# Seven block products instead of eight in the value projections of a two-layer trunk

## The chip, the cores and the metric

The kernel runs on one core of one Trainium2 chip. Its time is the device time of one execution in microseconds (us), and smaller is better. TensorE (PE) multiplies matrices, VectorE (DVE) and ScalarE (ACT) work elementwise, GpSimd (POOL) and SyncE (SP) mostly issue DMAs. Each engine runs its own instructions in the order in which the compiler wrote them down, and waits on semaphores for the others.

## The reference, cut to what matters

The model has two layers. Each adds a token mixer, a cross-attention on a memory and a squared-ReLU MLP to `x` (256 tokens, 2048 features). The part that changes is the attention:

```
h, mem_n = rms_norm(x, g_xattn[i]), rms_norm(mem, g_mem[i])        # 256 x 2048 each
q = (h @ w_q).reshape(.., 4 heads, 512)
k, v = split(mem_n @ w_kv, 2)                                      # v: 256 x 2048 = mem_n @ w_v
p = softmax(q k^T * 512**-0.5)                                     # per head, 256 x 256
x = x + (p v) @ w_o
```

The MLP is `x + square(relu(h @ w_up)) @ w_down`, with 8192 hidden features. All is float32.

## The kernel before, in words

**Number format.** Every float32 weight and activation is split in two parts of TensorE's faster float32 form: `split` lets ACT cast the high part (line 101, tile `whi` for weights) and DVE subtract it from the source (line 102, `wlo`). A product of two such numbers is three matmuls: high by high, high by low, low by high.

**Weights.** They stream from memory in chunks of 128 x 1024 floats (512 KB), loaded by SP into `wraw` (4 buffers, `wload`, line 118) and split by `wtile` into `whi` and `wlo` (3 buffers each). A chunk holds two k tiles of 128 by 512 output features (`KB = 2`), or, for the projections with transposed output (`gemm_feat`, used for q, k and the MLP's first matrix), four k tiles by 256 features (`FK = 4`).

**Plain product.** `gemm_tok` computes 256 tokens by 512 features: 8 chunks, 12 matmuls of 512 columns for each (2 k tiles, 2 token tiles, 3 parts). The value projection is four calls of it, one for each head; after each, the result is scaled by the memory's norm and split into `vh` and `vl` (lines 536 and 537) and weighted by the softmax of its head (24 matmuls of 256 columns, line 547), which gives `oT`.

**Seven-product form.** `gemm_seven` computes 256 tokens by two blocks of 512 features at once. For the first two chunks of each block (a 2 by 2 by 2 block product: two token tiles, two chunks, two feature blocks) it uses the scheme with seven block products instead of eight, each of 6 matmuls. It needs sums of the activation blocks (`token_sums`, lines 645 to 648, then a split) and of the weight blocks: DVE subtractions of two 128 x 1024 tiles (lines 718, 724, 729, 734), each split again. Products are numbered 1 to 7. The other six chunks of each block are plain (`direct`, 12 matmuls each). The code writes the products down as 5, 1, 2, a direct, 6, a direct, 7, a direct, 4, a direct, 3, then directs; `keep` (line 710) copies intermediate results out of PSUM, and `gather` adds results to `x`. Raw weights of the four special chunks are loaded into `ws`; the tile `run` holds the running difference of products 5, 6 and 4, while `ws` keeps the sources. The form is used for `w_o` in both attentions (two calls each) and for `w_down` in layer 1's MLP (seven calls).

**Order of the work.** The order on each engine is set at compile time by a scheduler that lets the work written down first go first, unless its inputs are not ready in its own model of time. `at(n, fn)` writes `fn` down n steps (`tick`, one for each weight chunk of a plain product) later. `mem_prep` prepares the transposed, scaled memory (`memT`) in four pieces as side work under the q projection of head 0; the k projection that follows reads its k tiles from 0 to 15.

Of the kernel before, what the change touches and what calls it, by code (L numbers as in the profile page):

```python
# [35 lines left out]
MAGIC = 12582912.0  # L36


class Trunk:
# [114 lines left out]
    def gemm_feat(self, act, w, n, dst):  # L154
# [4 lines left out]
        for kc in range(KT // FK):  # L159
            hi, lo = self.wtile(w, n, kc)  # L160
            for kk in range(FK):
                kt = kc * FK + kk
                st, en = kt == 0, kt == KT - 1
# [109 lines left out]
    def mem_prep(self, pool, layer):  # L273
# [192 lines left out]
    def attention(self, x, layer, cur, nxt):  # L466
# [3 lines left out]
        with tc.tile_pool(name="at", bufs=2, reuse_waits="tile") as ap:  # L470
# [5 lines left out]
            def proj(act, w, n, nm):  # L476
                h = ap.tile([P, 4, S], F32R, name=nm + "h")
                l = ap.tile([P, 4, S], F32R, name=nm + "l")
                for i in range(2):
                    z = ap.tile([P, 2, S], F32, name="z")  # L480
                    self.gemm_feat(act, w, 2 * n + i, z)
# [37 lines left out]
            for hd in range(HEADS):  # L519
                q = proj(hT, wq, hd, "q")  # L520
                self.flush()
                k = proj(memT, wk, hd, "k")
# [7 lines left out]
            for hd in range(HEADS):  # L530
                acc = self.gemm_tok(memT, wv, hd)
                vh = ap.tile([P, 2, HD], F32R, name="vh")
                vl = ap.tile([P, 2, HD], F32R, name="vl")
                for t in range(2):
                    r = self.rstd_mem[:, t:t + 1]
                    nc.scalar.activation(out=vh[:, t, :], in_=acc[:, t, :], func=AF.Copy, scale=r)
                    nc.vector.scalar_tensor_tensor(out=vl[:, t, :], in0=acc[:, t, :], scalar=r,
                                                   in1=vh[:, t, :].bitcast(F32), op0=ALU.mult, op1=ALU.subtract)
# [15 lines left out]
                if hd == 0:  # L554
                    for fp in range(2):
                        o = ap.tile([P, 2, S], F32, name="o", tag="e")
                        nc.scalar.copy(out=o, in_=ops[fp])
                        ops[fp] = o
                    sums = self.token_sums(ap.tile([P, KB * NB], F32, name="s", tag="qh"),
                                           lambda: ap.tile([P, 4, 2, P], F32R, name="sums", tag="kh"), *ops)  # L560

            nxt.start()
            count = iter(range(100))
            ws = lambda: ap.tile([P, KB * NB], F32, name="ws", tag=("ql", "qh")[next(count) % 2])
            run = lambda: ap.tile([P, KB * NB], F32, name="run", tag="kl")
            pair = {}

            def kept(i):
                if i in (1, 2):
                    return ap.tile([P, NB], F32, name="kept", tag="z")  # L570
                if i == 0:
                    pair[0] = ap.tile([P, 2, NB], F32, name="kept2", tag="kl")
                return pair[0][:, i // 3, :]
# [5 lines left out]
            for j in range(0, NCH, 2):  # L579
                self.gemm_seven((ws, run, kept), lambda kt, t: [f[:, kt, t * P:(t + 1) * P] for f in oT[:2]],  # L580
                                sums, wo, j, 0, gather)
# [4 lines left out]
    def mlp(self, x, layer, cur, nxt):  # L586
# [3 lines left out]
        with tc.tile_pool(name="ml", bufs=4, reuse_waits="tile") as mp:  # L590
            r2 = mp.tile([P, 32 if layer else 56], F32, name="r2", bufs=1)[:, 0:2]
            ws = lambda: mp.tile([P, KB * NB], F32, name="ws", bufs=4)
            sm = lambda: mp.tile([P, 4, 2, P], F32R, name="sums", bufs=2)
            run = lambda: mp.tile([P, KB * NB], F32, name="run", bufs=1)
            kept = lambda i: mp.tile([P, NB], F32, name="kept", bufs=4)
            for b in range(DFF // D):
                hid = []
                for n in range(NCH):
# [3 lines left out]
                    for i in range(2):  # L602
                        r = mp.tile([P, 2, S], F32, name="r", bufs=2)
# [5 lines left out]
                    if nxt.closing and n == 0:  # L609
                        sums = self.token_sums(ws(), sm, *rs)  # L610
# [11 lines left out]
                for n in range(NCH):  # L622
                    end = b == DFF // D - 1
                    if nxt.closing and not (end and n >= NCH - 2):
                        if n % 2 == 0:
                            self.gemm_seven((ws, run, kept), lambda kt, t: [f[:, kt % 4, t * P:(t + 1) * P]
                                                                            for f in hid[kt // 4]],
                                            sums, wd, n, b * KT, gather)
# [24 lines left out]
    def gemm_seven(self, tiles, token, sums, w, n0, k0, gather):  # L653
# [6 lines left out]
        kc0 = k0 // KB  # L660
        ws, run, kept = tiles
        raw, half = {}, lambda t: t.rearrange("p (k c) -> p k c", k=KB)

        def fetch(i, j):
            t = ws()
            self.fed = nc.sync.dma_start(out=half(t), in_=w[n0 + j, kc0 + i]).ins
            raw[i, j] = t
# [7 lines left out]
        begun = set()  # L675

        def into(key, kts, left, hi, lo, end=False):
            out = banks[key]
            for kk in kts:
                ah, al = left(kk)  # L680
                mm = lambda s, m, e: nc.tensor.matmul(out, s, m, start=key not in begun, stop=e, skip_group_check=True)  # L681
                mm(ah, hi[:, kk, :], False)
                begun.add(key)
                mm(ah, lo[:, kk, :], False)
                mm(al, hi[:, kk, :], True)

        def block(key, t, i, src, end=False):
            into(key, range(KB), lambda kk: token(KB * i + kk, t), *parts(src), end)

        def summed(key, k, src, end=False):  # L690
            into(key, range(KB), lambda kk: [f[:, k, kk, :] for f in sums], *parts(src), end)

        todo = {j: list(range(2, KT // KB)) for j in range(2)}

        def direct(j, first):
# [3 lines left out]
            for t in (first, 1 - first):  # L699
                into((t, j), range(KB), lambda kk: token(KB * kc + kk, t), hi, lo)  # L700
                yield
            self.tick()

        def whole(*a):
            for _ in direct(*a):
                pass
# [5 lines left out]

        acc = [self.psA.tile([P, 2, NB], F32, name="acc") for _ in range(2)]
        banks = {(1, 0): acc[0][:, 0], (0, 1): acc[0][:, 1], (0, 0): acc[1][:, 0], (1, 1): acc[1][:, 1]}
        for i, j in ((0, 0), (0, 1), (1, 0), (1, 1)):
            fetch(i, j)
        run = run()
        v.tensor_tensor(out=run, in0=raw[0, 1], in1=raw[0, 0], op=ALU.subtract)
        summed((0, 1), 0, run, True)
        block((1, 0), 0, 0, raw[0, 0], True)  # L720
        m5, m1 = keep((0, 1), 0), keep((1, 0), 1)
        block((0, 0), 0, 1, raw[1, 0])
        whole(1, 1)
        v.tensor_tensor(out=run, in0=raw[1, 1], in1=run, op=ALU.subtract)
        summed((1, 0), 1, run, True)
        gather(0, n0, m1)
        u2 = keep((1, 0), 2)
        whole(1, 1)
        v.tensor_tensor(out=raw[0, 1], in0=raw[1, 1], in1=raw[0, 1], op=ALU.subtract)
        summed((1, 0), 2, raw[0, 1], True)  # L730
        gather(0, n0 + 1, u2)
        u3 = keep((1, 0), 3)
        whole(0, 0)
# [667 lines left out]
```

## Time and profile before

| | |
|---|---|
| time, median of 3 runs | 2835.14 us (2832.22 to 2835.55) |
| profiled execution, its own time | 2834.88 us |
| its span, first to last instruction | 2832.0 us |
| TensorE busy | 2798.7 us (99%) |
| VectorE busy | 1958.4 us (69%) |
| ScalarE busy | 1393.7 us (49%) |
| mean granted TensorE clock | 0.998 of 2.4 GHz |

Matmuls are pipelined and their ends are modelled: a matmul's "busy" or mean time is not the time by which the next one is held up. What counts is the distance from one start to the next. In the chain of waits a line "20.20 PE acc L149 x89" is 89 matmuls that started one after the other within 20.20 us.

### The profile page before, as it was taken

Reading aid. Unit: us, or ns where it says so; the run is one execution under the profiler, and the core shown is the slowest. Engines: PE = TensorE matmul, PEld = TensorE weight load, DVE = VectorE, ACT = ScalarE, POOL = GpSimd, SP = SyncE. Lnnn points to the kernel's source line nnn. Section 1 sums busy time; section 2 is a strip of 40 time slices with the busy share of each in tenths; the row PEclk is TensorE's granted clock in tenths of the full one; section 3 lists DMA queues with packets and bytes.
Section 4 is the critical chain, followed back from the end, with each engine's and each line's share of the span. In section 5 each row is a group of like instructions: output and inputs, shape, how many; then the busy total and the mean of one; then the engine's idle time right before and its main releaser. Section 6 shows DMA issues by size and latency. Waiting matters only on the chain.

```text
span 2832.0 us, 39687 instructions
## 1 busy us (share of the span) xinstructions
PE 2798.7 (99%) x15172; PEld 2346.5 (83%) x15172; DVE 1958.4 (69%) x2707; ACT 1393.7 (49%) x1801; POOL 200.3 (7%) x374
## 2 busy tenths in 40 slices
PE   9999999999999999999999999999999999999998
PEld 7888888888888888888777788888888888888886
DVE  6855655578878788787567666556676767667665
ACT  5545544454544444444455445444454545445453
POOL 0100000001022222222011000000000000000000
PEclk9999999999999999999999999999999999999999
DMA  8766665657677777777879766566556576575755
GB/s 287 238 199 204 193 180 186 180 156 237 195 220 215 224 223 220 217 223 211 236 249 286 217 213 200 175 187 192 171 179 217 163 223 186 170 217 163 221 160 155
DMA packets 180847, 579.55 MB, mean 205 GB/s; under 512 B 37440, under 2 KB 39664, under 8 KB 179888
## 3 DMA queue, kind: packets, MB, share of 16 engines
q1 hardware_dynamic: 142304, 513.34, 59.0%
q0 software_dynamic: 38208, 63.62, 8.3%
q8 instruction: 118, 1.93, 0.3%
q14 instruction: 73, 0.60, 0.1%
q10 hardware_dynamic: 144, 0.07, 0.0%
HBM read 553.88 MB, written 22.94 MB: 204 GB/s over the span
## 4 chain that ended last, share of the span: by engine, by line
PE 88%; DVE 4%; DMA 4%; issue 2%; ACT 1%; POOL 0%; DVEq 0%; POOLq 0%; SPq 0%; ACTq 0%
PE acc L166 23%; PE acc L149 21%; PE acc L681 14%; PE acc L168 12%; PE acc L766 4%; PE acc L765 4%; PE acc L764 4%; DVE wlo L102 2%; DMA Kd<-kd 1%; PE ps L547 1%; PE ps L490 1%; DMA wraw<-in_f_w_down 1%; PE ps L149 1%; ACT whi L101 1%; PE ps L217 1%
## 5 line engine op out<-in xcount | busy, mean ns | idle before, releaser
L102 DVE TENSOR_TENSOR wlo<-wraw,whi 128x1024 fp32r<-128x1024 f32 x908 | 1108.5, 1222 | 660.8 <-ACT whi L101 656.8
L101 ACT CAST whi<-wraw 128x1024 fp32r<-128x1024 f32 x908 | 955.0, 1052 | 1128.6 <-PE acc L166 360.3
L166 PE MATMUL acc<-act,whi 128*128 128x512 f32 x3072 | 1082.9, 396 | 0.9 <-ACT whi L101 0.8
L168 PE MATMUL acc<-act,wlo 128*128 128x256 f32 x3072 | 865.0, 282 | 1.7 <-DVE wlo L102 1.5
L166 PEld LDWEIGHTS acc<-act,whi 128*128 128x128 f32 x3072 | 576.0, 188 | 133.9 <-ACT whi L101 1.7
L149 PE MATMUL acc<-whi,act 128*128 128x512 f32 x1984 | 623.5, 393 | 8.6 <-ACT whi L101 6.9
L168 PEld LDWEIGHTS acc<-act,wlo 128*128 128x128 f32 x3072 | 580.4, 189 | 7.0 <-DVE wlo L102 3.4
L149 PEld LDWEIGHTS acc<-whi,act 128*128 128x128 f32 x1984 | 373.0, 189 | 86.6 <-ACT whi L101 6.9
L149 PE MATMUL acc<-wlo,act 128*128 128x512 f32 x992 | 387.7, 391 | 2.0 <-DVE wlo L102 2.0
L149 PEld LDWEIGHTS acc<-wlo,act 128*128 128x128 f32 x992 | 187.0, 189 | 40.5 <-DVE wlo L102 2.9
L765 PE MATMUL acc<-wlo,hh 128*128 128x512 f32 x544 | 215.1, 395 | 0.2 <-DVE wlo L102 0.2
L764 PE MATMUL acc<-whi,hh 128*128 128x512 f32 x544 | 214.5, 394 | 0.0
L766 PE MATMUL acc<-whi,hl 128*128 128x512 f32 x544 | 214.4, 394 | 0.0
L681 PE MATMUL acc<-wlo,hh 128*128 128x512 f32 x378 | 147.6, 390 | 1.7 <-DVE wlo L102 1.6
L681 PE MATMUL acc<-whi,hh 128*128 128x512 f32 x378 | 147.6, 390 | 0.5
L681 PE MATMUL acc<-whi,hl 128*128 128x512 f32 x378 | 147.2, 389 | 0.0
L681 PE MATMUL acc<-whi,act 128*128 128x512 f32 x432 | 135.8, 389 | 0.0
L765 PEld LDWEIGHTS acc<-wlo,hh 128*128 128x128 f32 x544 | 102.2, 188 | 24.4 <-DVE wlo L102 1.5
L766 PEld LDWEIGHTS acc<-whi,hl 128*128 128x128 f32 x544 | 102.2, 188 | 22.8 <-issue 1.6
L764 PEld LDWEIGHTS acc<-whi,hh 128*128 128x128 f32 x544 | 102.2, 188 | 22.2 <-issue 0.4
L681 PEld LDWEIGHTS acc<-whi,act 128*128 128x128 f32 x432 | 80.8, 188 | 16.7 <-ACT kept L710 0.2
L681 PEld LDWEIGHTS acc<-wlo,hh 128*128 128x128 f32 x378 | 71.0, 188 | 17.9 <-DVE wlo L102 3.1
(320 smaller groups left out, 2562.5 us busy)
## 6 DMA issues: line engine op xcount, KB each, us to landing
wraw<-in_f_w_up SPq DMA_DIRECT2D x256, 512.0 KB, 4.2
wraw<-in_f_w_down SPq DMA_DIRECT2D x228, 512.0 KB, 4.3
wraw<-in_a_w_in SPq DMA_DIRECT2D x64, 512.0 KB, 4.5
wraw<-in_x_w_q SPq DMA_DIRECT2D x64, 512.0 KB, 3.7
wraw<-in_x_w_k SPq DMA_DIRECT2D x64, 512.0 KB, 3.7
wraw<-in_x_w_v SPq DMA_DIRECT2D x64, 512.0 KB, 3.7
wraw<-in_b_w_out SPq DMA_DIRECT2D x64, 512.0 KB, 4.4
wraw<-in_x_w_o SPq DMA_DIRECT2D x48, 512.0 KB, 3.9
```

What stands on the lines that cost most here:

```text
L101: self.nc.scalar.copy(out=hi, in_=src)
L102: self.nc.vector.tensor_tensor(out=lo, in0=src, in1=hi.bitcast(F32), op=ALU.subtract)
L149: nc.tensor.matmul(out[t], pairs[m][0][:, kt, sl], pairs[m][1][:, kk, :], start=st and m == 0, stop=en and m == 2)
L166: nc.tensor.matmul(acc[:, f, :], hi[:, kk, sl], both[:, kt].rearrange("p a s -> p (a s)"), start=st, stop=False, skip_group_check=True)
L168: nc.tensor.matmul(acc[:, f, 0:S], lo[:, kk, sl], ah[:, kt, :], start=False, stop=en, skip_group_check=True)
L217: nc.tensor.transpose(pt[:, kk, t * P:(t + 1) * P], src[:, t, c:c + P], self.ident)
L490: mm = lambda s, m, b, e: nc.tensor.matmul(sc[:, t, :], s, m, start=b, stop=e, skip_group_check=True)
L547: mm = lambda s, mv, b, e: nc.tensor.matmul(op[:, k, :], s, mv, start=b, stop=e, skip_group_check=True)
L681: mm = lambda s, m, e: nc.tensor.matmul(out, s, m, start=key not in begun, stop=e, skip_group_check=True)
L764: nc.tensor.matmul(acc[:, t, :], ah[:, kt % 4, sl], hi[:, kk, :], start=st, stop=False)
L765: nc.tensor.matmul(acc[:, t, :], ah[:, kt % 4, sl], lo[:, kk, :], start=False, stop=False)
L766: nc.tensor.matmul(acc[:, t, :], al[:, kt % 4, sl], hi[:, kk, :], start=False, stop=en)
```

## The change

The value projections of both attentions use the seven-product form too, two heads per call, with the activation sums of the memory (`mem_sums`). `gemm_seven` is replaced by `gemm_pair`, which takes the order of the products as a list and an optional function `end` for the finished blocks. What differs:

- Product 1 comes before product 5; the directs come in another order at the end of the list.
- The tile `run` is gone: each weight difference is written over a raw chunk, 5, 6 and 4 over chunk (0,0), 7 over chunk (0,1). So a difference can only be formed when the product that read the chunk before has been split.
- In the value projections `end` adds a kept partial result (for three of the four blocks), scales and splits into `vh` and `vl`. The weighting of a pair's two heads is written down 1 and 2 steps into the next pair: for heads 2 and 3 that is the first pair of `w_o`.
- `mem_prep`'s pieces come in the order 1, 2, 3, 0. Piece 0 is scaled in place, split as a whole and summed. The k projection runs over its k tiles in the order 4 to 15, then 0 to 3.
- In the MLPs `ws` has 5 buffers instead of 4, and the tile `r` shares the buffers of `kept`.

```diff
+ONE_GROUP = "1 5 2 d1 6 d1 7 d0 4 d1 3 d0 d1 d0 d1 d0 d0".split()
...
-    def gemm_feat(self, act, w, n, dst):
+    def gemm_feat(self, act, w, n, dst, kcs=range(KT // FK)):
-        for kc in range(KT // FK):
+        for kc in kcs:
...
         def piece(j):
             m = pool.tile([P, 4, S], F32, name="memc")
             self.nc.gpsimd.dma_start(out=m, in_=self.a["mem_t"][j])
-            self.scale_chunk(m, 4 + layer, act, j)
-        self.side += [lambda j=j: piece(j) for j in range(NCH)]
+            if j:
+                return self.scale_chunk(m, 4 + layer, act, j)
+            for k in range(4):
+                self.nc.vector.tensor_scalar(out=m[:, k, :], in0=m[:, k, :], scalar1=self.gcol[:, 4 + layer, k:k + 1],
+                                             scalar2=None, op0=ALU.mult)
+            self.split(act[0][:, 0:4, :], act[1][:, 0:4, :], m)
+            self.mem_sums = self.token_sums(pool.tile([P, KB * NB], F32, name="s", tag="vh"),
+                                            lambda: pool.tile([P, 4, 2, P], F32R, name="msums", tag="memc"),
+                                            m[:, 0:2], m[:, 2:4])
+        self.side += [lambda j=j: piece(j) for j in (1, 2, 3, 0)]
...
-            for hd in range(HEADS):
-                acc = self.gemm_tok(memT, wv, hd)
-                vh = ap.tile([P, 2, HD], F32R, name="vh")
-                vl = ap.tile([P, 2, HD], F32R, name="vl")
-                for t in range(2):
+            homes = iter(("vh", "vl") * 2 + ("ql", "qh") * 6)
+            ws = lambda: ap.tile([P, KB * NB], F32, name="ws", tag=next(homes))
+            ends = ap.tile([P, 2, NB], F32, name="ends", tag="kl")
+            kept = lambda i: ap.tile([P, NB], F32, name="kept", tag="z") if i in (1, 2) else ends[:, i // 3, :]
+            def values(h0):
+                vs, more = [], {}
+                def end(t, n, src):
+                    if not vs:
+                        vs.extend([ap.tile([P, 2, HD], F32R, name=nm) for nm in ("vh", "vl")] for _ in range(2))
+                    part = more.pop((t, n), None)
+                    if part is not None:
+                        nc.vector.tensor_tensor(out=part, in0=src, in1=part, op=ALU.add)
+                        src = part
+                    vh, vl = (f[:, t, :] for f in vs[n - h0])
                     r = self.rstd_mem[:, t:t + 1]
+                    nc.scalar.activation(out=vh, in_=src, func=AF.Copy, scale=r)
+                    nc.vector.scalar_tensor_tensor(out=vl, in0=src, scalar=r, in1=vh.bitcast(F32),
+                                                   op0=ALU.mult, op1=ALU.subtract)
+                self.gemm_pair((ws, kept), token(memT), [self.mem_sums], wv, h0, 0,
+                               lambda t, n, part: more.update({(t, n): part}), ONE_GROUP, end)
+                return vs
...
+            for h0 in range(0, HEADS, 2):
+                vs = values(h0)
+                for i in range(2):
+                    self.at(1 + i, lambda hd=h0 + i, v=vs[i]: weighted(hd, *v))
...
+        def summed(key, k, i, j, minus=None):
+            for q in groups:
+                src = raw[q, i, j]
+                if minus is not None:
+                    src = raw[q, 0, minus]
+                    v.tensor_tensor(out=src, in0=raw[q, i, j], in1=src, op=ALU.subtract)
...
+            if step == "1":
+                block((1, 0), 0, 0, 0)
+            elif step == "5":
+                summed((0, 1), 0, 0, 1, 0)
+                part[5], part[1] = keep((0, 1), 0), keep((1, 0), 1)
+            elif step == "2":
+                block((0, 0), 0, 1, 0)
+            elif step == "6":
+                summed((1, 0), 1, 1, 1, 0)
+                add(0, 0, part[1])
+                part[6] = keep((1, 0), 2)
+            elif step == "7":
+                summed((1, 0), 2, 1, 1, 1)
+                add(0, 1, part[6])
+                part[7] = keep((1, 0), 3)
+                v.tensor_tensor(out=part[7], in0=part[7], in1=part[5], op=ALU.add)
+            elif step == "4":
+                summed((1, 0), 4, 1, 0, 0)
+                add(1, 1, part[7])
+            elif step == "3":
+                summed((0, 1), 3, 1, 1)
```

## Rows read from the trace of the kernel before

**Rows 1.** The page's first part: busy time, share of the span and number of instructions of each engine.

```profile
PE 2798.7 (99%) x15172; PEld 2346.5 (83%) x15172; DVE 1958.4 (69%) x2707; ACT 1393.7 (49%) x1801; POOL 200.3 (7%) x374
```

**Rows 2.** The chain of waits in order of time (start, length, what), from the value projection of layer 0 (L149 with weighting, L547) into its `w_o` (L681).

```profile
504.19 20.20 PE acc L149 x89
...
574.22 0.60 PE ps L547 x4
...
577.23 1.67 PE ps L547 x14
578.90 42.69 PE acc L681 x188
```

**Rows 3.** The page's costliest groups: one kind of matmul of the plain and one of the seven-product form (count, busy us, mean ns of one).

```profile
L149 PE MATMUL acc<-whi,act 128*128 128x512 f32 x1984 | 623.5, 393 | 8.6 <-ACT whi L101 6.9
...
L681 PE MATMUL acc<-whi,act 128*128 128x512 f32 x432 | 135.8, 389 | 0.0
```

**Rows 4.** Busy time of the engines in the stretches of layer 0's value projection and of its `w_o`.

```profile
477.00:577.00 100.00, 100.00 (x486) 83.15 (x485) 58.41 (x63) 46.07 (x55) 0.10 (x1) 1.00 0.59 178
577.00:633.00 56.00, 56.00 (x263) 46.63 (x262) 44.22 (x47) 31.82 (x40) 0.00 (x0) 1.00 0.52 161
```

**Rows 5.** Groups of DVE and ACT instructions by line and shape (count, busy us, mean ns of one, idle before).

```profile
L102 DVE TENSOR_TENSOR wlo<-wraw,whi 128x1024 fp32r<-128x1024 f32 x908 | 1108.5, 1222 | 660.8 <-ACT whi L101 656.8
L101 ACT CAST whi<-wraw 128x1024 fp32r<-128x1024 f32 x908 | 955.0, 1052 | 1128.6 <-PE acc L166 360.3
...
L729 DVE TENSOR_TENSOR ws<-ws 128x1024 f32<-128x1024 f32 x11 | 13.5, 1224 | 8.2 <-DMA ws<-in_f_w_down 5.6 <-DMA ws<-in_x_w_o 2.5
...
L537 DVE SCALAR_TENSOR_TENSOR vl<-acc,rstd_mem,vh 128x512 fp32r<-128x512 f32 x16 | 12.0, 748 | 9.0 <-ACT vh L536 9.0
...
L577 DVE TENSOR_TENSOR x<-kept,x 128x512 f32<-128x512 f32 x12 | 8.2, 685 | 0.6 <-ACT kept L710 0.6
L738 DVE TENSOR_TENSOR kept<-kept 128x512 f32<-128x512 f32 x11 | 7.5, 683 | 0.0
...
L236 DVE SCALAR_TENSOR_TENSOR act<-memc,gcol,act 128x256 fp32r<-128x256 f32 x48 | 20.6, 477 | 6.4 <-ACT act L235 6.4
...
L508 DVE TENSOR_SCALAR e<-e,rsm 128x256 f32<-128x256 f32 x16 | 4.9, 351 | 0.3
...
L646 DVE TENSOR_TENSOR ws<-ws,r 128x256 f32<-128x256 f32 x4 | 1.7, 416 | 0.0
L710 ACT COPY kept<-acc 128x512 f32<-128x512 f32 x44 | 24.7, 588 | 8.1 <-PE acc L681 8.1
```

**Rows 6.** DVE's instructions in order of time at the seam between the two `w_down` pairs of one hidden block in layer 1: the low part of product 5, product 6's difference, two gathers, the low part of product 1, two gathers, the low part of product 2, that of the first direct, a gather, the low part of product 6.

```profile
2243.48 1.22 DVE L102 TENSOR_TENSOR wlo<-run,whi 128x1024 fp32r<-128x1024 f32 x1 [1.50 <-ACT whi L101]
2244.74 1.23 DVE L724 TENSOR_TENSOR run<-ws,run 128x1024 f32<-128x1024 f32 x1
2245.89 1.40 DVE L619 SCALAR_TENSOR_TENSOR x<-acc,r,x 128x512 f32<-128x512 f32 x2
2247.56 1.23 DVE L102 TENSOR_TENSOR wlo<-ws,whi 128x1024 fp32r<-128x1024 f32 x1 [0.28 <-ACT whi L101]
2248.71 1.40 DVE L619 SCALAR_TENSOR_TENSOR x<-acc,r,x 128x512 f32<-128x512 f32 x2
2250.03 1.22 DVE L102 TENSOR_TENSOR wlo<-ws,whi 128x1024 fp32r<-128x1024 f32 x1
2251.16 1.22 DVE L102 TENSOR_TENSOR wlo<-wraw,whi 128x1024 fp32r<-128x1024 f32 x1
2252.29 0.75 DVE L619 SCALAR_TENSOR_TENSOR x<-kept,r,x 128x512 f32<-128x512 f32 x1
2252.96 1.22 DVE L102 TENSOR_TENSOR wlo<-run,whi 128x1024 fp32r<-128x1024 f32 x1
```

**Rows 7.** PE's matmuls where the two `w_down` pairs of one hidden block begin: at the start of product 2 of the first pair, and within product 2 of the second.

```profile
2207.16 0.39 PE L681 MATMUL acc<-whi,hl 128*128 128x512 f32 x1
2207.68 0.50 PE L681 MATMUL acc<-whi,hh 128*128 128x512 f32 x1
...
2250.36 0.39 PE L681 MATMUL acc<-whi,hh 128*128 128x512 f32 x1
2251.30 0.50 PE L681 MATMUL acc<-wlo,hh 128*128 128x512 f32 x1 [0.55 <-DVE wlo L102]
```

**Rows 8.** DVE's instructions in order of time in layer 0's `w_o`: two weight differences of the second pair, formed while the first still runs, and the low parts of products 2 and 6 of the second pair.

```profile
592.10 1.22 DVE L718 TENSOR_TENSOR run<-ws 128x1024 f32<-128x1024 f32 x1
...
598.80 1.23 DVE L729 TENSOR_TENSOR ws<-ws 128x1024 f32<-128x1024 f32 x1 [0.96 <-DMA ws<-in_x_w_o]
...
620.74 1.21 DVE L102 TENSOR_TENSOR wlo<-ws,whi 128x1024 fp32r<-128x1024 f32 x1
...
624.60 1.22 DVE L102 TENSOR_TENSOR wlo<-run,whi 128x1024 fp32r<-128x1024 f32 x1
```

**Rows 9.** ACT's instructions in order of time in layer 1: the last piece of the memory after its DMA, then the copies out of PSUM after q's second half and after the first half of the k projection of head 0.

```profile
1756.84 0.91 ACT L235 ACTIVATE act<-memc,gcol 128x256 fp32r<-128x256 f32 x2 [2.43 <-DMA memc<-in_mem_t]
...
1760.34 0.57 ACT L171 COPY z<-acc 128x512 f32<-128x512 f32 x1
...
1769.38 0.58 ACT L171 COPY z<-acc 128x512 f32<-128x512 f32 x1
```

More of the change, by code (lines that the diff above doesn't have):

```diff
@@ L553, in attention @@
                     self.split(oT[0][:, kt:kt + 2, :], oT[1][:, kt:kt + 2, :], op)
[L554 to L560, printed above, removed]
-            nxt.start()
[L563 to L573, printed above, removed]
+                if hd:
+                    return
+                for fp in range(2):
+                    o = ap.tile([P, 2, S], F32, name="o", tag="e")
+                    nc.scalar.copy(out=o, in_=ops[fp])
+                    ops[fp] = o
+                sums.append(self.token_sums(ap.tile([P, KB * NB], F32, name="s", tag="kl"),
+                                            lambda: ap.tile([P, 4, 2, P], F32R, name="sums", tag="kh"), *ops))
+            sums = []
+            for h0 in range(0, HEADS, 2):
+                vs = values(h0)
+                for i in range(2):
+                    self.at(1 + i, lambda hd=h0 + i, v=vs[i]: weighted(hd, *v))
+            nxt.start()
             def gather(t, n, part):
@@ L579, in attention @@
             for j in range(0, NCH, 2):
-                self.gemm_seven((ws, run, kept), lambda kt, t: [f[:, kt, t * P:(t + 1) * P] for f in oT[:2]],
-                                sums, wo, j, 0, gather)
+                self.gemm_pair((ws, kept), token(oT), sums, wo, j, 0, gather, ONE_GROUP)
                 for n in (j, j + 1):
@@ L651, in token_sums, with gemm_pair, fetch @@
         return sh, sl
-    def gemm_seven(self, tiles, token, sums, w, n0, k0, gather):
+    def gemm_pair(self, tiles, token, sums, w, n0, k0, gather, order, end=None):
         nc = self.nc
         v = nc.vector
[L660 to L667, printed above, removed]
+        kc0, groups = k0 // KB, range(len(sums))
+        ws, kept = tiles
+        raw, begun, half = {}, set(), lambda t: t.rearrange("p (k c) -> p k c", k=KB)
+        def fetch(q, i, j):
+            raw[q, i, j] = t = ws()
+            self.fed = nc.sync.dma_start(out=half(t), in_=w[n0 + j, kc0 + 2 * q + i]).ins
         def parts(src):
@@ L711, in keep, with add @@
             return t
+        def add(t, j, part):
+            gather(t, n0 + j, part)
         acc = [self.psA.tile([P, 2, NB], F32, name="acc") for _ in range(2)]
         banks = {(1, 0): acc[0][:, 0], (0, 1): acc[0][:, 1], (0, 0): acc[1][:, 0], (1, 1): acc[1][:, 1]}
[L715 to L733, printed above, removed]
@@ L734, in gemm_seven @@
-        v.tensor_tensor(out=run, in0=raw[1, 0], in1=run, op=ALU.subtract)
-        block((1, 0), 1, 1, run)
-        whole(1, 1)
-        summed((0, 1), 3, raw[1, 1])
-        v.tensor_tensor(out=u3, in0=u3, in1=m5, op=ALU.add)
-        whole(0, 0)
-        gather(1, n0 + 1, u3)
-        while len(todo[0]) > 1 or len(todo[1]) > 1:
-            j = len(todo[1]) > len(todo[0])
-            whole(j, j)
+        for i, j in ((0, 0), (0, 1), (1, 1), (1, 0)):
+            for q in groups:
+                fetch(q, i, j)
@@ new lines, in gemm_pair @@
+        part, after = {}, []
+        for step in order:
+            if step == "1":
[19 more added lines that the diff above has]
+                summed((0, 1), 3, 1, 1)
+            else:
+                for _ in direct(int(step[1]), int(step[1])):
+                    pass
@@ L748, in gemm_seven @@
             for t, j in keys:
-                gather(t, n0 + j, banks[t, j])
+                (end or gather)(t, n0 + j, banks[t, j])
         for e in ends:
```

61 lines of the change are left out of this document (27 added, 34 removed).

## The prediction, made before the changed kernel ran

> **What bounds the kernel now.** I read the busy shares first, then the chain of waits in order of time, then single stretches of DVE's and PE's instructions. TensorE is busy all along, the others are not [rows 1]. That share alone proves little, because a matmul's end is modelled, so I look at starts. In the plain value projection 89 matmuls of 512 columns follow each other within 20.20 us, in `w_o`'s seven-product form 188 within 42.69 us: 227 ns each in both [rows 2]. So both forms already run at TensorE's own pace, without holes. The weighting is no hole either: at the seam into `w_o` the scheduler strews its matmuls between those of the next product [rows 2]. In both stretches PE is busy throughout, while DVE has 42 of 100 us free under the value projection and 12 of 56 us under `w_o` [rows 4]. A matmul removed here is therefore worth its 227 ns, as long as DVE and ACT deliver the split weights in time. Where they don't is seen in `w_down`: PE waits inside product 2 of a second pair for its low part, from 2250.36 to 2251.30, which is 0.71 us more than the 0.23 of one matmul, and 0.29 us where a first pair comes to product 2 [rows 7].
>
> **What is removed on PE.** A pair of heads costs 2 x 8 x 12 = 192 matmuls now. The new form costs 7 products of 6 and 12 directs of 12: 186. Two attentions with two pairs each: 4 x 6 = 24 matmuls fewer, 24 x 0.227 = 5.45 us. The weighting keeps its matmuls, `w_o` and `w_down` keep theirs. The price is the distance between starts, not the mean of 390 ns that the groups show [rows 3], which would make 9.4 us.
>
> The Trainium skill ("TensorE: Matmul & The Clock Gate", section on the back-to-back issue gap) gives about 131 ns for a sustained matmul of 512 columns, by which the saving would be an estimated 3.1 us; this kernel's start-to-start distance contradicts it, and the measurement decides.
>
> **What is added on DVE and ACT.** Per value pair: three more weight chunks to split (19 instead of 16), four differences of 128 x 1024, one sum of kept parts and three additions in `end`. With 1.22, 1.22 and 0.685 us [rows 5] this is 7 x 1.22 + 4 x 0.685 = 11.3 us of DVE per pair, 22.6 per attention. The 42 us that DVE has free in that stretch take it [rows 4]. On ACT it is three casts of 1.05 and three `keep` copies of 0.59 [rows 5], 5 us of the 54 free. On average nothing becomes the bound; what counts is where DVE's work falls together.
>
> **Seams of the value pairs.** I take the seam of rows 6 as the pattern. From the start of the first low part (2243.48) to when PE wants the low part of product 2 (2250.36 + 0.23 = 2250.59) there are 7.1 us. DVE had to do three low parts, one difference and four gathers in them: at the distances of these rows, 1.13 for a tile of 1024 and 0.67 for a gather, 4 x 1.13 + 4 x 0.67 = 7.2 us, and 7.8 with its waits for ACT. The 0.7 us too many are the hole of rows 7. The new value seam (pair into pair, and second pair into `w_o`) has the same low parts, again one difference (product 5's now, since it must wait for product 1's split), and the four ends: three additions and four `vl` (0.61 and 0.67 from start to start, as 0.745 gives 0.67 here), 4.5 + 1.8 + 2.7 = 9.0, with the same waits 9.6 us: a hole of 2.5 us if all of it stands ahead of product 2's low part. But three of the four `vl` read a kept tile, not PSUM, and hold up no matmul except the weighting; put behind, 2.0 us leave the window and 0.5 remain. At the seam from head 3 into `w_o` two `vl` cost no hole at all, since weighting filled it [rows 2]. Bounds 0 and 2.5; I take 0.5, four times: +2.0 us. The weighting, written down one and two steps into the next pair, then gives DVE 24 x 0.12 = 2.9 us of PE work per head to catch up.
>
> **First value pair.** It follows a k projection as a first `w_down` pair follows the MLP's first matrix, so I take the hole of rows 7, 0.3 us, twice: +0.6 (0 to 1.0 each, as the softmax of head 3 also wants DVE there).
>
> **Differences in place, in all pairs.** Before, products 5 and 7 had their differences formed far ahead (at 592.10 and 598.80, while the second pair's product 2 gets its low part at 620.74) [rows 8]. Now chunk (0,0) must first be split for product 1 and then for 5, so the differences of 5, 6 and 7 fall into the busy zone of the pair itself. What is late next is product 6. In the second `w_down` pair of a block its difference would start where the gather stands now (2252.29), end at 2253.4, the cast (1.05) at 2254.5 and the low part at 2255.7; PE comes to it after product 2 (2252.4) and a direct (12 x 0.227) at 2255.2 and wants the low part at 2255.4: a hole of 0.3 us [rows 6]. Three such pairs: +0.9 (0 to 1.1 each). In first pairs DVE has time, as the matrix before asks one chunk in 2.8 us. The second `w_o` pair has two differences more (2.3 us) in a zone where DVE already goes from instruction to instruction, from the low part of 2 to that of 6 [rows 8]; transposes of the next norm fill part of such holes. 0.3 us, twice: +0.6 (0 to 2.3 each). The existing `w_down` holes, taken alike in the four first and three second pairs, 4 x 0.29 + 3 x 0.71 = 3.3 us, I leave as they are (bounds: gone, or as much again).
>
> **Memory sums and rotated k tiles.** Piece 0 costs 4 scalings of 0.35, a split of 1.22, four sums of about 0.42 and another split: 5.5 us of DVE instead of 4 x 0.48 = 1.9 [rows 5]. This stands beside the q and k projections. In layer 1 the last piece reaches ACT at 1756.84, right after its DMA. The k projection's first half ends at about 1769.3 and lasts 32 x 0.347 = 11.1 us (a matmul of 512 and one of 256 columns, 0.227 + 0.12), so its last quarter begins at about 1766.5 [rows 9]. In the new order that quarter is the one that needs piece 0; ready at about 1756.8 + 1.4 + 1.05 + 1.2 = 1760.5, it has 6 us to spare. Without that rotation it would be wanted at 1758.2 and cost 2.3 us. Counted at 0 (to 0.5 each). Buffers: `ws` and `kept` in the MLP have as much room as before or more, the weight bytes are the same; 0.
>
> **Sum.** -5.45 + 2.0 + 0.6 + 0.9 + 0.6 = -1.35 us on the profiled execution's 2834.88: 2833.5 us. That execution lies 0.26 us under the median of the three runs, which doesn't matter here. About 0.2% (5.7 us) is what a measurement of this kernel can tell from no change, so even the whole saving of 5.45 us lies at that limit.
>
> **The rivals.**
> (a) All seams close, and the order with product 1 first (it needs only one raw chunk) also closes holes in `w_down`: -5.45 to -8.75 us, 2829.4 down to 2826.1. For it speaks that the first `w_o` pair has no hole at all in spite of `vl` work; against it, that the second `w_down` pair's hole comes from DVE's load, which the change doesn't lighten. Chance 0.25.
> (b) Slower: in the value seams the scheduler puts every `vl` in front, since they are written down before the next pair's splits. Then the four seams cost up to 2.5 us each, 10 us, and with the other terms' +2.1 the time is 2834.9 - 5.45 + 12.1 = 2841.5. It decides once a seam costs more than about 2.3 us, or 1.5 us with `w_o`'s second pairs at 2 us each. For it: rows 6 show gathers in front of low parts that PE waits for. Chance 0.15.
> (c) The saving is made and given back in full, so the change does nothing: holes of 5.45 us in sum, 2834.9. It is part of the case "same", whose chance is 0.60 (holes between 1 and 11 us).
>
> Likeliest: 2833.5. The low end, 2828.0, takes in most of (a); the high end, 2840.5, reaches just short of (b)'s price. Chances: faster by over 0.2% 0.25, within 0.2% 0.60, slower 0.15.
>
> **What the new profile would show.** The matmul count must fall by 24 to 15148, with 227 ns between starts. In each value seam I look for the order on DVE: low parts of 5 and 2 against `vl`; a start-to-start distance over 0.23 us in product 5 or 2 is the hole. In `w_o`'s second pairs and `w_down`'s, product 6 should wait for its low part by some 0.3 us. The k projection of head 0 should wait for nothing of the memory. The forecast is wrong if DVE's order at the seams is better or worse than taken, if the early raw chunks of the first value pair come late, or if a `keep` copy that waits for a kept tile blocks the casts queued behind it on ACT.

## The result and the profile after

The changed kernel takes 2848.07 us (median of 6 runs, 2847.24 to 2850.16), the kernel before 2835.11 on the same chip: ratio 1.0050, 95% interval 1.0037 to 1.0063. It is slower by 13 us, where 2833.5 was forecast. The page's first part answers [rows 1]:

```profile
PE 2802.6 (98%) x15148; PEld 2343.4 (82%) x15148; DVE 2004.1 (70%) x2763; ACT 1414.9 (50%) x1825; POOL 200.6 (7%) x374
```

The 24 matmuls are gone, and the spacing is still 227 ns. So TensorE waits more. The view of PE's waits (line, releaser, us in total, times, longest) shows for whom. The matmuls of the seven-product form, line 681 before, had one row there:

```profile
PE acc L681 <- DVE wlo L102: 1.6, 3, 0.6
```

Their line 702 in the changed kernel has more:

```profile
PE acc L702 <- ACT whi L103: 5.5, 10, 1.0
...
PE acc L702 <- DVE kept L174: 2.7, 4, 0.9
...
PE acc L702 <- DVE wlo L104: 1.7, 3, 0.6
PE acc L702 <- DVE x L641: 1.5, 3, 0.5
PE acc L702 <- ACT ends L734: 0.9, 2, 0.5
```

These 12.3 us count from modelled ends of matmuls; a hole is longer when read from start to start, less the 0.23 us of one matmul, and so I read holes below. I also cut both traces at the first matmul of each stage. The change's own stages give +12.6 us: value projection and `w_o` +2.9 (layer 0) and +3.2 (layer 1), though 12 matmuls (2.72 us) are gone from each, and `w_down` +6.5. The rest adds 1.0.

**The value seam** (first pair into second, layer 0). DVE in order of time, from the low part of product 1 (515.05) to that of product 2 (524.17):

```profile
515.05 1.23 DVE L104 TENSOR_TENSOR wlo<-ws,whi 128x1024 fp32r<-128x1024 f32 x1 [1.49 <-ACT whi L103]
516.31 1.22 DVE L716 TENSOR_TENSOR ws<-ws 128x1024 f32<-128x1024 f32 x1
517.46 0.74 DVE L560 SCALAR_TENSOR_TENSOR vl<-acc,rstd_mem,vh 128x512 fp32r<-128x512 f32 x1
518.12 0.68 DVE L555 TENSOR_TENSOR kept<-acc,kept 128x512 f32<-128x512 f32 x1
518.72 1.22 DVE L716 TENSOR_TENSOR ws<-ws 128x1024 f32<-128x1024 f32 x1
519.85 0.74 DVE L560 SCALAR_TENSOR_TENSOR vl<-kept,rstd_mem,vh 128x512 fp32r<-128x512 f32 x1
520.51 0.68 DVE L555 TENSOR_TENSOR kept<-acc,kept 128x512 f32<-128x512 f32 x1
521.11 0.68 DVE L555 TENSOR_TENSOR ends<-acc,ends 128x512 f32<-128x512 f32 x1
521.71 1.21 DVE L104 TENSOR_TENSOR wlo<-ws,whi 128x1024 fp32r<-128x1024 f32 x1
522.84 0.74 DVE L560 SCALAR_TENSOR_TENSOR vl<-kept,rstd_mem,vh 128x512 fp32r<-128x512 f32 x1
523.50 0.74 DVE L560 SCALAR_TENSOR_TENSOR vl<-ends,rstd_mem,vh 128x512 fp32r<-128x512 f32 x1
524.17 1.22 DVE L104 TENSOR_TENSOR wlo<-ws,whi 128x1024 fp32r<-128x1024 f32 x1
```

and PE, where product 5 (`msums`) and product 2 begin:

```profile
520.57 0.40 PE L702 MATMUL acc<-whi,msums 128*128 128x512 f32 x1
521.94 0.47 PE L702 MATMUL acc<-whi,act 128*128 128x512 f32 x1 [0.97 <-ACT whi L103]
522.54 0.39 PE L576 MATMUL ps<-pTh,vh 128*128 128x256 f32 x1
```

Two differences (line 716) go ahead of every low part that PE wants: that of product 5 (516.31) and that of product 7 (518.72), whose turn comes only after products 2, 6 and two directs. (Product 7's difference was written over a raw chunk before, too, L729 in [rows 5]. But product 5's difference has to read that chunk first, and it now waits until product 1's chunk is split.) DVE runs without a gap; PE waits 1.14 us (520.57 to 521.94) and 0.38 us (521.94 to 522.54, a matmul of the weighting, whose `vh` ACT ends at 522.49). For the first hole the profile names ACT's cast, but the last addition, which frees a bank of PSUM (521.11 + 0.68 = 521.79), ends 0.15 us before product 2 starts; runs below tell these two apart. The seam into `w_o` has the same two holes, 1.14 and 0.38, as have both seams of layer 1: 4 x 1.52 = 6.1 us.

**The seam between two `w_down` pairs**, DVE and PE of after, to be laid beside [rows 6] and [rows 7]:

```profile
2250.57 1.22 DVE L104 TENSOR_TENSOR wlo<-ws,whi 128x1024 fp32r<-128x1024 f32 x1 [1.49 <-ACT whi L103]
2251.83 1.23 DVE L716 TENSOR_TENSOR ws<-ws 128x1024 f32<-128x1024 f32 x1
2252.97 1.41 DVE L641 SCALAR_TENSOR_TENSOR x<-acc,r,x 128x512 f32<-128x512 f32 x2
2254.29 1.22 DVE L716 TENSOR_TENSOR ws<-ws 128x1024 f32<-128x1024 f32 x1
2255.42 1.41 DVE L641 SCALAR_TENSOR_TENSOR x<-acc,r,x 128x512 f32<-128x512 f32 x2
2256.74 2.35 DVE L104 TENSOR_TENSOR wlo<-ws,whi 128x1024 fp32r<-128x1024 f32 x2
```

```profile
2256.08 0.39 PE L702 MATMUL acc<-whi,sums 128*128 128x512 f32 x1
2256.97 0.47 PE L702 MATMUL acc<-whi,hh 128*128 128x512 f32 x1 [0.50 <-DVE x L641]
2258.01 0.51 PE L702 MATMUL acc<-wlo,sums 128*128 128x512 f32 x1 [0.57 <-DVE wlo L104]
```

Before, this stretch held one difference between two low parts, and the gathers had their place behind it. Now there are two, and they push back both the gathers that empty PSUM (hole 0.66 us) and the low parts (0.81 us). A third hole of 0.31 follows: 1.78 in place of the 0.71 of [rows 7]. First pairs lose too, 0.74 to 1.06 in place of 0.29. There three differences (2208.43, those of 5 and 7, and 2212.11, that of 6) and the low parts of 5 and 2 stand ahead of the last piece of the MLP's first matrix, which DVE has to take out of PSUM (line 174). PE stands from 2214.16 to 2215.13. Which of them matters there, E9 will tell:

```profile
2208.43 2.48 DVE L716 TENSOR_TENSOR ws<-ws 128x1024 f32<-128x1024 f32 x2
...
2214.39 0.69 DVE L174 TENSOR_TENSOR kept<-acc,kept 128x512 f32<-128x512 f32 x1
```

**The second `w_o` pair.** [rows 8] had two differences far ahead of it. Now all four lie inside:

```profile
616.06 1.22 DVE L716 TENSOR_TENSOR ws<-ws 128x1024 f32<-128x1024 f32 x1
...
618.40 1.22 DVE L716 TENSOR_TENSOR ws<-ws 128x1024 f32<-128x1024 f32 x1
...
624.92 1.21 DVE L716 TENSOR_TENSOR ws<-ws 128x1024 f32<-128x1024 f32 x1
...
634.67 0.69 DVE L762 TENSOR_TENSOR ends<-ends 128x512 f32<-128x512 f32 x1 [0.44 <-ACT ends L734]
635.28 1.22 DVE L716 TENSOR_TENSOR ws<-ws 128x1024 f32<-128x1024 f32 x1
...
637.66 1.23 DVE L104 TENSOR_TENSOR wlo<-ws,whi 128x1024 fp32r<-128x1024 f32 x1 [0.57 <-ACT whi L103]
```

The last one, product 4's, is queued behind an addition for which DVE waits for ACT (634.67), and its low part comes at 637.66. In the kernel before these two stood at 626.87 and 631.78, while both kernels have a low part at the same time (620.74 in [rows 8], 620.73 now; but it was product 2's before and is product 5's now, product 2's follows 1.1 us later):

```profile
626.87 1.22 DVE L734 TENSOR_TENSOR run<-ws,run 128x1024 f32<-128x1024 f32 x1
...
631.78 1.23 DVE L102 TENSOR_TENSOR wlo<-run,whi 128x1024 fp32r<-128x1024 f32 x1
```

PE has holes of 0.23, 0.21, 0.61, 0.35 and 0.72 us between 627.8 and 638.6, 2.1 us per layer.

### The profile page after: what moved, and what is told of

Read it like the earlier page. It is cut to its first block, busy times and chain, and to the rows that moved or that the text cites. A ratio compares the mean times of both kernels' runs of the same rounds, so it can differ in the third digit from the quotient of the medians.

```text
span 2845.4 us, 39743 instructions
## 1 busy us (share of the span) xinstructions
PE 2802.6 (98%) x15148; PEld 2343.4 (82%) x15148; DVE 2004.1 (70%) x2763; ACT 1414.9 (50%) x1825; POOL 200.6 (7%) x374
## 4 chain that ended last, share of the span: by engine, by line
PE 87%; DVE 6%; ACT 2%; DMA 2%; issue 2%; POOL 0%; DVEq 0%; ACTq 0%; SPq 0%; POOLq 0%
PE acc L168 23%; PE acc L702 19%; PE acc L151 14%; PE acc L170 12%; PE acc L793 4%; PE acc L792 4%; PE acc L791 4%; DVE wlo L104 2%; ACT whi L103 1%; PE ps L500 1%; PE ps L576 1%; PE ps L151 1%; PE ps L219 1%; PE ps L1050 0%; DMA wraw<-in_f_w_down 0%
## 5 line engine op out<-in xcount | busy, mean ns | idle before, releaser
L104 DVE TENSOR_TENSOR wlo<-wraw,whi 128x1024 fp32r<-128x1024 f32 x892 | 1090.1, 1223 | 660.8 <-ACT whi L103 655.9
L103 ACT CAST whi<-wraw 128x1024 fp32r<-128x1024 f32 x892 | 937.9, 1052 | 1100.8 <-PE acc L168 360.9
L151 PE MATMUL acc<-whi,act 128*128 128x512 f32 x1472 | 464.4, 393 | 8.5 <-ACT whi L103 6.8
L151 PEld LDWEIGHTS acc<-whi,act 128*128 128x128 f32 x1472 | 277.9, 189 | 68.0 <-ACT whi L103 6.8
L151 PE MATMUL acc<-wlo,act 128*128 128x512 f32 x736 | 287.7, 392 | 2.5 <-DVE wlo L104 2.5
L702 PE MATMUL acc<-whi,act 128*128 128x512 f32 x864 | 276.4, 392 | 6.5 <-ACT whi L103 5.5
L702 PEld LDWEIGHTS acc<-whi,act 128*128 128x128 f32 x864 | 162.2, 188 | 46.2 <-ACT whi L103 9.3
L702 PE MATMUL acc<-wlo,act 128*128 128x512 f32 x432 | 168.6, 390 | 0.0
L151 PEld LDWEIGHTS acc<-wlo,act 128*128 128x128 f32 x736 | 138.7, 188 | 31.7 <-DVE wlo L104 3.9
L103 ACT CAST whi<-ws 128x1024 fp32r<-128x1024 f32 x105 | 110.4, 1051 | 107.0 <-PE acc L702 65.0
L104 DVE TENSOR_TENSOR wlo<-ws,whi 128x1024 fp32r<-128x1024 f32 x105 | 127.8, 1221 | 35.7 <-ACT whi L103 35.7
L792 PEld LDWEIGHTS acc<-wlo,hh 128*128 128x128 f32 x544 | 102.6, 189 | 23.3 <-issue 1.0
```

The lines of the kernel that those rows point to most:

```text
L103: self.nc.scalar.copy(out=hi, in_=src)
L104: self.nc.vector.tensor_tensor(out=lo, in0=src, in1=hi.bitcast(F32), op=ALU.subtract)
L151: nc.tensor.matmul(out[t], pairs[m][0][:, kt, sl], pairs[m][1][:, kk, :], start=st and m == 0, stop=en and m == 2)
L702: nc.tensor.matmul(banks[key], s, m[:, kk, :], start=key not in begun, stop=m is hi and s is al, skip_group_check=True)
L792: nc.tensor.matmul(acc[:, t, :], ah[:, kt % 4, sl], lo[:, kk, :], start=False, stop=False)
```

## The experiments

Theory A: the order of DVE's work is at fault. With differences formed in place (line 716) and product 1 first, they can't be formed early; they fall in front of low parts and PSUM readers that TensorE wants. Theory B: the value form itself is at fault, by `vl` work at its seams. Others: less room in the MLP's buffers, more DVE load. The table gives the stages of each kernel's profiled execution against before (us, cut at first matmuls, worked out by me); "rest" also holds stages whose code is the same, and it moves by up to 4.4 us between kernels (in part by the clock, as the last section shows), so a single stage is read, and the verdict is the ratio. Chips differ between groups of runs; each ratio is against the kernel before on the same chip.

| kernel | v + w_o, layer 0 | layer 1 | w_down | rest | median | ratio to before, 95% |
|---|---|---|---|---|---|---|
| after | +2.9 | +3.2 | +6.5 | +1.0 | 2848.1 | 1.0050 [1.0037, 1.0063] |
| e1_old_wo_wd | -1.0 | -0.7 | -0.3 | +0.2 | 2831.9 | 0.9987 [0.9978, 0.9996] |
| e2_plain_values | +3.3 | +3.5 | +6.4 | +2.1 | 2846.1 | 1.0040 [1.0028, 1.0053] |
| e3_run_first | -1.0 | -2.5 | +1.4 | +4.4 | 2831.6 | 0.9988 [0.9980, 0.9997] |
| e4_late_split | +0.3 | +0.9 | +6.3 | +0.0 | 2842.7 | 1.0025 [1.0016, 1.0035] |
| e5_run_late | -2.8 | -1.6 | +0.7 | +2.7 | 2831.3 | 0.9989 [0.9980, 0.9998] |
| e6_old_late | -2.4 | -2.2 | -0.3 | +3.2 | 2828.6 | 0.9980 [0.9970, 0.9990] |
| e7_own_tile_1_first | -1.4 | +0.2 | +3.2 | +2.6 | 2837.2 | 1.0011 [1.0002, 1.0021] |
| e8_old_buffers | +2.9 | +3.1 | +6.3 | +2.8 | 2847.9 | 1.0052 [1.0038, 1.0066] |
| e9_no_difference_7 | -1.5 | +0.6 | +4.1 | +3.9 | 2838.2 | 1.0011 [1.0001, 1.0020] |
| e10_add_behind_4 | +1.9 | +2.1 | +6.7 | +1.8 | 2845.8 | 1.0043 [1.0028, 1.0057] |
| e11_run_late_add | -1.9 | -0.6 | +0.9 | +2.9 | 2833.2 | 0.9989 [0.9980, 0.9999] |

**The two halves of the change.** E1 keeps the new value projection and gives `w_o` and `w_down` the old code and buffers; E2 is the reverse.

```
-   self.gemm_pair((ws, kept), token(oT), sums, wo, j, 0, gather, ONE_GROUP)
+   self.gemm_seven((ws, run, kept7), token(oT), sums[0], wo, j, 0, gather)     # E1, alike in mlp
```

> Value projections in the new form as in the changed kernel, but w_o and w_down go back to the old seven-product code (product 5 first, differences in a tile of their own, 4 raw buffers). Theory A, the differences formed in place push DVE work into the pair: w_down gives back 6.5 us and the second w_o pairs about 4 us, time about 2837, w_down stretches as before within 0.3 us each. Theory B, the value seams carry the loss: only 2 to 3 us come back, about 2845.

> Value projections and memory preparation go back to the plain form of before; w_o and w_down keep the new order with differences in place. Theory A: the loss stays, about 2845 (2835 + 6.5 for w_down + 4 for the second w_o pairs). Theory B: about 2837, since without value seams little is lost.

E2 loses nearly all that the full change loses, without any value form in it; E1 wins 3.3 us. The first part of E1's page:

```profile
PE 2795.7 (99%) x15148; PEld 2342.5 (83%) x15148; DVE 2002.5 (71%) x2763; ACT 1415.4 (50%) x1825; POOL 200.2 (7%) x374
```

E1 has the same number of instructions on PE, DVE and ACT as the changed kernel, and DVE is as long busy (2002.5 and 2004.1 us), yet it is 16 us faster. So it isn't DVE's load; it is the order.

**Place and order.** E3 gives the differences of 5, 6 and 4 a tile of their own and puts product 5 first; E7 gives the tile alone. Both also have the MLP's buffers of before, which E8 tests by themselves; the other novelties of `gemm_pair` (order of the fetches and of the directs, place of the addition) stay.

```
-ONE_GROUP = "1 5 2 d1 6 ...
+ONE_GROUP = "5 1 2 d1 6 ...                                          # E3, not E7
-   src = raw[q, 0, minus]
-   v.tensor_tensor(out=src, in0=raw[q, i, j], in1=src, op=ALU.subtract)
+   old, src = (raw[q, 0, 0] if k == 0 else run, run) if minus == 0 else (raw[q, 0, 1],) * 2
+   v.tensor_tensor(out=src, in0=raw[q, i, j], in1=old, op=ALU.subtract)
```

> All pairs of the changed kernel, values too, but product 5 comes first and the differences of 5, 6 and 4 have a tile of their own again, so 5 and 7 can be formed early. Theory A: w_down as before, second w_o pairs as before, value seams shorter by one or two differences (1.1 us each): about 2835, at best 2832. Theory B (order doesn't matter, the ends of the values do): about 2845.

> As the run with product 5 first, but with product 1 first as in the changed kernel; the differences keep their own tile. Separates the order from the place. If the place decides (differences of 5 and 7 can be formed ahead), w_down stays within 0.7 us of before in each stretch and the time is 2832 to 2834. If the order decides, w_down's stretches are 2 us longer again and the time is about 2842.

E3 takes 6.5 to 1.4 us in `w_down`, E7 to 3.2: the tile is worth 3.3 us and the order another 1.8. The ratio falls from 1.0050 to 1.0011 by the tile and to 0.9988 with the order. DVE at the `w_down` seam of E3 has one difference again:

```profile
2245.44 1.22 DVE L719 TENSOR_TENSOR run<-ws,run 128x1024 f32<-128x1024 f32 x1
2246.58 1.40 DVE L644 SCALAR_TENSOR_TENSOR x<-acc,r,x 128x512 f32<-128x512 f32 x2
2248.26 1.23 DVE L104 TENSOR_TENSOR wlo<-ws,whi 128x1024 fp32r<-128x1024 f32 x1 [0.27 <-ACT whi L103]
2249.40 1.41 DVE L644 SCALAR_TENSOR_TENSOR x<-acc,r,x 128x512 f32<-128x512 f32 x2
2250.72 1.22 DVE L104 TENSOR_TENSOR wlo<-ws,whi 128x1024 fp32r<-128x1024 f32 x1
```

That is the sequence of [rows 6], and PE's hole there is back at 0.71 us (0.94 from start to start). E8 gives the changed kernel the MLP's old buffers:

> The changed kernel with the MLP's buffers of before (4 for raw chunks, the tile r with two of its own). If buffers have no part in the loss of w_down, its stretches stay 1.7 to 2.3 us longer than before: about 2848. If waiting for a raw chunk or a kept tile is the cause, they come back: about 2842.

Nothing moves (1.0052, `w_down` +6.3): the buffers have no part in it.

**One subtraction.** E9 leaves out the difference of product 7 alone.

```
    if minus is not None:
        src = raw[q, 0, minus]
+   if minus == 0:
        v.tensor_tensor(...)              # the difference; shortened
```

> The changed kernel without the subtraction that forms product 7's difference (the product takes the raw chunk as it is; everything else is left). If DVE's order at the seams is the cause, this one instruction counts for much: it stands unneeded ahead of the low parts that TensorE wants at each value seam, in each second w_o pair and in each w_down pair, at 1.13 us a time. The four value seams should then lose most of their 1.14 us (4.5 together), the three second w_down pairs about 1.1 of their 1.8 us, the four first ones about 0.4 each: some 9 us, 2838 to 2840. If the seams wait for ACT or for a bank of PSUM instead, or if only DVE's total load counted (16 subtractions among 2763 instructions), the time stays within 2 us of 2848.

2838.2 us, ratio 1.0011: inside what was expected, but not split as expected. `w_down` regains 2.4 us (I had 4.9), value projections and `w_o` 7.0 (4.4 in layer 0, 2.6 in layer 1). At the value seam the low part of product 5 now stands at 519.85 instead of 521.71, and of the holes only one is left:

```profile
522.39 0.39 PE L702 MATMUL acc<-whi,msums 128*128 128x512 f32 x1
523.08 0.47 PE L702 MATMUL acc<-whi,act 128*128 128x512 f32 x1 [0.30 <-DVE ends L555]
```

0.46 us, released by the addition that empties the bank. In the second `w_o` pair of layer 0 product 4's difference moved ahead of the addition too (631.10), which is the gain that I had not counted; in layer 1 it stayed behind it (2084.48), and holes of 0.62, 0.76 and 0.72 us stand there (0.61, 0.35 and 0.72 in the changed kernel). In `w_down` only second pairs gain. A first pair keeps its hole of 0.74 us (2209.74 to 2210.71): where product 7's difference stood, DVE now waits 1.19 us for ACT's cast of product 5's difference. So in first pairs it is the differences of 5 and 6 that are late, not that of 7; with a tile of their own (E7) the hole is 0.29 again, as before. The kernel has 15 subtractions fewer (2748 DVE instructions, not 2763) and 17 us less of DVE's busy time; as E1 has shown that this load alone costs nothing, what counts is what they stood in front of. One thing stays mixed: without the instruction the scheduler also ordered the rest anew.

**Late split.** E4 writes the scaling and splitting of the three kept blocks one step later, so only additions stand at the seam. E6 is E4 on E1, E5 is E4 on E3.

```
+   def finish(vh, vl, src=src, r=...): (scale, split)
-   (scale, split)
+   finish(*cut) if part is None else self.at(0, lambda f=finish, c=cut: f(*c))
```

> The changed kernel, with the scaling and splitting into vh and vl of the three blocks that have a kept part written down one step into the next pair, so that they stand behind the splits of products 1, 5, 2 and the first direct. If the vl work in front of the low parts makes the value seams' holes (1.5 us each, four of them), 4 to 6 us come back, 2842 to 2844, with the v and w_o stretch shorter by 2 to 3 us per layer. If the holes come from the differences alone: 2848, no change.

> The run with the old code in w_o and w_down, plus the later scaling and splitting. Its seam between the two value pairs still has differences in place and a hole of 1.5 us (1.14 and 0.38); late splitting took such a hole from 1.5 to 0.5 us in the changed kernel. So 1 us less per layer: about 2830. If the hole comes from the differences alone: 2831.9.

> Both remedies: product 5 first with a tile of its own for the differences in all pairs, and the scaling and splitting of blocks with a kept part one step later. If the two act on separate holes, the value seams lose another 0.4 us each and the time is 2829 to 2831. If the early differences already left the ends of the values enough of DVE, nothing changes: 2831.6.

E4 gains 2.6 and 2.3 us in the two value and `w_o` stretches, and its seam has only this hole left, the same 0.47 us and the same releaser as in E9:

```profile
520.75 0.40 PE L708 MATMUL acc<-whi,msums 128*128 128x512 f32 x1
521.45 0.47 PE L708 MATMUL acc<-whi,act 128*128 128x512 f32 x1 [0.30 <-DVE ends L555]
```

So of the seam's 1.52 us about 1.05 are DVE work that could stand elsewhere, `vl` or product 7's difference, whichever is moved. Theory B is right only so far: `vl` costs this where a difference stands beside it. E6 has the lowest time and ratio of all, 2828.6 us, 0.9980 [0.9970, 0.9990], and beats both kernels; its interval overlaps those of E1, E3 and E5. All of its waits in the seven-product forms (line 721 the old form, 820 the new one) and in the weighting (line 582):

```profile
PE acc L721 <- DVE wlo L104: 1.6, 3, 0.6
...
PE acc L820 <- DVE ends L555: 0.6, 2, 0.3
PE ps L582 <- ACT vh L559: 0.4, 2, 0.2
```

E5 doesn't gain over E3 (0.9989 and 0.9988); its stretch of layer 0 is 1.8 us better, that of layer 1 1.0 worse. Both differences are one hole in a first value pair, in E3 of 1.75 us in layer 0 (490.20 to 492.18), in E5 of 0.98 in layer 1. DVE waits there for a raw chunk to land, to form product 7's difference early, and the scaling of head 3's softmax, which PE wants next, is queued behind (E3):

```profile
489.44 1.23 DVE L719 TENSOR_TENSOR ws<-ws 128x1024 f32<-128x1024 f32 x1 [1.70 <-DMA ws<-in_x_w_v]
```

E11 has the same hole in both layers (0.94 and 1.95). Without it the stretches of E3 and E5 would be 2.5 to 2.8 us shorter than before.

**The addition ahead of product 4.** E10 moves one line of the changed kernel behind product 4; E11 does so in E5.

```
     summed((1, 0), 4, 1, 0, 0)
+    v.tensor_tensor(out=part[7], in0=part[7], in1=part[5], op=ALU.add)     # was in step 7
     add(1, 1, part[7])
```

> The changed kernel with one instruction moved: the addition of product 5 to product 7 is written behind product 4 instead of ahead of it. In the second w_o pair DVE stands at this addition until ACT has copied product 7 out of PSUM, and product 4's difference is queued behind it (635.28). If that queue makes product 4 late, the holes of 0.35 and 0.72 us at 637 to 638.6 close: 1.0 us per layer, 2.0 to 2.5 in all, 2845.5 to 2846. If product 4's difference is late for want of its tile, which product 6 has to leave first, nothing changes: 2848.

> The kernel e5_run_late (a tile of its own for the differences, product 5 first, late scale and split) with the addition moved as in e10. What is left of e5 against the kernel before is up to 0.4 us in each w_down stretch. If that is the addition's place, w_down goes back to 0.0 and the time is 2830; if it comes from something else (the order of the fetches), nothing changes: 2831.3.

E10 regains 1.0 us in each layer's stretch, as expected of the queue, and the holes of 0.35 and 0.72 us are gone. Product 4's difference now starts at 634.52 and the addition follows, without a wait:

```profile
634.52 1.22 DVE L716 TENSOR_TENSOR ws<-ws 128x1024 f32<-128x1024 f32 x1
635.65 0.69 DVE L764 TENSOR_TENSOR ends<-ends 128x512 f32<-128x512 f32 x1
```

The median is 2.3 us lower (2845.8), but the intervals of the two ratios overlap, so the stage is the evidence. E11 changes nothing (0.9989 as E5, `w_down` +0.9): the up to 0.4 us per `w_down` stretch that E5 has over the kernel before is not this addition. What it is stays open; the order of the fetches (chunk (1,1) now comes before (1,0)) and DVE's other order are left.

## Why the prediction was wrong, point by point

- **24 matmuls at 227 ns, -5.45 us: right.** The count is 15148 and the spacing the same. E6 shows it net: -2.4 and -2.2 us in the two stretches that lost 12 matmuls each, with holes of 0.47 us (the bank in PSUM) and 0.38 us (ACT's `vh`) still in the two seams of each; the kernel before had gaps of 0.1 us of its own around its weighting. The figure in the Trainium skill ("TensorE: Matmul & The Clock Gate", section on the back-to-back issue gap), 131 ns, would have allowed no more than an estimated 1.6 each; the runs contradict it for this kernel.
- **Value seams, +2.0 us: 6.1 measured.** The window was counted right in `vl` and additions, and I was right that three `vl` could go behind; one went ahead of the bank's addition and low part all the same, and with it the difference of product 7, which I didn't count at all. This is rival (b)'s mechanism at 1.52 of its 2.5 us a seam, just where I said that it decides. It is not the value form's alone: with the old `w_o` behind the same value pair (E1) the seam into `w_o` has 0.42 instead of 1.52.
- **Differences in place, +0.9 and +0.6: the step that failed.** I listed product 6's difference as the next late one and asked when it would be ready. What came late at the seams was the work behind product 7's difference, formed as soon as its operands were there, at a time when DVE had no idle slot. Measured: `w_down` +6.5, and 2.1 us of holes in each second `w_o` pair. For first `w_down` pairs I took nothing, as DVE has time there; but the last stretch, which has a first pair alone, lost 0.47 us, and 0.01 in E1. There product 5's difference waits for product 1's split, and DVE reaches the accumulation that empties PSUM too late; E9 shows that product 7's has no part in it.
- **Product 4** was not in the sum: the diff moves the addition from behind product 3 into step 7, ahead of product 4, and I read past it. E10 prices it at 1.0 us per layer.
- **First value pair, +0.6: nothing measured.** No hole over 0.25 us stands there.
- **ACT's added work** was counted short: a value pair has four `keep` copies, not three, and the 54 us free are for two pairs. ACT is 21 us longer busy than before (1414.9 and 1393.7); no conclusion rested on it.
- **Memory sums, rotated k tiles, buffers, 0: right.** The q and k stages, cut at first matmuls, differ by -0.01 and -0.19 us; for the buffers E8 shows it.

With measured terms the sum is -5.45 + 6.1 + 6.5 + 4.2 = +11.4 us against +12.6 in these stages. About 1.2 us of smaller holes and 1.0 in the other stages are not placed.

## What to carry to other kernels

When a change makes an operand's storage do double duty, ask of each instruction that it delays by a dependency not only when it is wanted but what it will now stand in front of; an in-order engine that is 70% busy on average can cost the full length of an instruction at every seam. Count every instruction that is ready in a seam, also those whose result is wanted later. Early has its price as well: in E3 an early difference waited for its DMA, and everything behind it on the engine waited along. Change a storage scheme and an algorithm in separate steps: the seven-product value projection alone, with a late split, is worth 0.2% here (E6), and the new form of the `w_o` and `w_down` pairs alone, storage, order and all, costs 0.4% (E2).

## What the runs showed that I had not expected

The MLP's first matrix in layer 1 alternates matmuls of 512 and 256 columns in unchanged code, yet it ran at two paces while PE had no hole. A window of 90 us inside its first stretch (first figures: length, then PE's busy time and number of matmuls; the granted clock stands behind POOL) in the kernel before:

```profile
2114.30:2204.30 90.00, 90.00 (x527) 79.42 (x526) 66.11 (x88) 47.11 (x63) 0.00 (x0) 1.00 0.65 205
```

and in the changed one:

```profile
2119.80:2209.80 90.00, 90.00 (x518) 78.22 (x517) 62.56 (x86) 45.95 (x63) 0.00 (x0) 1.00 0.64 211
```

The clock is 1.00 in both. Cut at first matmuls, this stretch lasts 90.6 us in before, E2, E4, E6, E7, E8, E10 and E11 and 92.1 us in after, E1, E3, E5 and E9; which it is goes with no part of the change. What sets the pace stays open. The granted clock moves other stages of unchanged code. Apart from the very end it reads 0.50, that is 1.2 of 2.4 GHz, in one short stretch in the kernel before (from 1543.9, in layer 1's mixer), and in three in the changed one (from 1375.0, at the end of layer 0's MLP, and from 1480.8 and 1545.7). In the first of these, ahead of which PE started nothing from 1371.81 to 1373.64, matmuls of 512 columns start mostly 0.43 us apart. Eight of them take 3.49 us instead of 1.82, a loss of 1.7:

```profile
1375.05:1378.45 3.40, 3.40 (x11) 2.72 (x9) 1.63 (x2) 3.37 (x8) 0.00 (x0) 0.50 0.78 306
```

No run has such a stretch in the value projections, `w_o` or `w_down`. With these, the 1.5 us of the two paces, an opening stage that varied by up to 3.2 us and layer 0's MLP (-2.3 to +2.4 us), all of the same or nearly the same code, single profiled executions settle nothing below some 3 us over the whole span, and stages have to be read one by one.
